# Seven block products in eight of the 22 row pairs of two down projections, with a later load and fewer dummies

## The chip, the cores and the metric

The kernel runs on one core of a Trainium2 chip. The metric is the device time of one execution in microseconds (us), as the median of several runs. TensorE (PE) multiplies, VectorE (DVE), ScalarE (ACT) and GpSimd (POOL) do the elementwise work, SyncE (SP) issues the transfers.

## The reference

One decoder layer on x of 256 tokens by 1024 features, in float32:

```
x <- LN1(alpha*x + 0.5*FFN1(x))
x <- LN2(alpha*x + W_out(sum_b sigmoid(g_b(x)) * P_b(mixer_b(x))))
x <- LN3(alpha*x + 0.5*FFN2(x))
FFN(x) = (silu(x @ w_gate) * (x @ w_up)) @ w_down      # 1024 -> 2816 -> 1024
```

The three mixers are a sliding-window attention, a block-sparse attention that at this length looks at its own block alone, and a cross-attention into 256 memory tokens `mem`, whose keys and values are `mem @ w_mem_kv + b`. alpha is 2 to the power 1/4. The change touches both FFNs and the time at which `mem` is loaded.

## The kernel before

Every weight is loaded once, as a chunk of 128 partitions x 2048 columns (1 MB), in the order in which `plan` lists them: for each FFN eleven gate and up chunks in turn, then eleven down chunks; between the FFNs those of the mixers. Each float32 operand is split in two parts of the type float32r: ScalarE casts the high part (`split`, L131), VectorE subtracts it for the low part (L132). A product is three matmuls (`product`, L187 to L189): high x high, high x low, low x high. So a chunk passes through SP (L153), ScalarE, VectorE and PE. `weights(key, ahead)` loads up to six chunks ahead and cuts up to two ahead. Three staging tiles (`raws`) hold loaded chunks; four slots each of `whi` and `wlo` (`parts`) hold cut ones, and a slot is written again when PE has read it for the last time. The order on SP is the program's own; on the other engines a scheduler orders the instructions when the kernel is built, and each engine then runs its list in that order. Only the first chunk is in program order on all of them.

In the gate and up loop of `ffn` the weights are stationary and the tokens move: for each feature block k one matmul of 512 columns (both parts of x) at L209 and one of 256 at L211. `gated` makes h = silu(g) * u * 0.5, and h is split into `hh` and `hl`. Chunk 0 of FFN 1 is worked in five groups of k as its pieces land (`FIRST`); after the second group `keep_warm(20)` puts 20 matmuls on a zero tile (L263) into PE's order, as 44 do at the start of the kernel.

In the down stage (`per_token`) h is stationary and the weights move. A down chunk holds two feature rows j of 128 by 1024 columns; for each of two token tiles t (128 tokens) and each half of the columns, `product` adds to one PSUM bank: 2 x 2 x 2 x 3 = 24 matmuls of 512 columns. There are eight banks. In FFN 2 the second half of t = 1 is cut into two banks of 256 columns (`ends`). The last three chunks are held back, so that all of t = 0 is finished before t = 1; then `normalize` takes alpha * resid + bank (L402), the statistics (L404 to L411) and the affine part (L415, L419) while PE works on t = 1. After FFN 1 PE goes on with the keys of mem (chunk mk), a transpose of the normalised x1 into x1T, the values of mem (mv), another transpose, and the projections of x1T (qa0, qa1, v0 and on).

`mem` is loaded by `hook_2` in chunk 7 of FFN 1 through a staging tile of `raws`, and split into `memT`, which has the tags C and E. The tag X1 belongs to x1. In FFN 2 the gate and up products of chunks 0 and 1 come first, by another way, and their h is turned and split in `hook_lead` at chunk 3, so `ffn` starts at chunk 2.

Of the kernel before, what the change touches and what calls it, by code (L numbers as in the profile page):

```python
# [17 lines left out]
P = 128  # L18
# [17 lines left out]
def plan():  # L36
# [79 lines left out]
def hybrid_layer(ctx: ExitStack, tc: tile.TileContext, a: dict, out: bass.AP):  # L116
# [39 lines left out]
    def part_to(n):  # L156
        while done["part"] <= min(n, len(chunks) - 1):
            i = done["part"]
            load_to(i)
            raw, how = raw_of.pop(i), chunks[i][1]  # L160
            if how:
                t = "1" if how == "leadg" else "2"
                hi = acts.tile([P, 2048], F32R, name="lhi", tag="A" + t)
                lo = acts.tile([P, 2048], F32R, name="llo", tag="B" + t)
            else:
                hi = parts.tile([P, 2048], F32R, name="whi")
                lo = parts.tile([P, 2048], F32R, name="wlo")
# [3 lines left out]
            part_of[i] = (hi, lo)  # L171
            done["part"] += 1

    def weights(key, ahead=2):
# [141 lines left out]
    def per_token(keys, lhs, keep, after, ahead=2, between=None, ends=HALVES):  # L316
# [23 lines left out]
        for t in range(2):  # L340
# [7 lines left out]
            after(t, [(*c, ps) for c, ps in zip(spans[t], py[t])])  # L348

    def gated(g, u):  # L350

# [5 lines left out]

    def ffn(n, x, after, start=0, hooks={}, h=None, ends=HALVES):
        hh, hl = h or (halves("hh", ("A1", "A2")), halves("hl", ("B1", "B2")))
        for c in range(start, NC):  # L360
            if c in hooks:
# [4 lines left out]
            for ks in FIRST if n == 1 and c == 0 else [range(KD)]:  # L366
                for key in ("g", "u"):
# [9 lines left out]
                    if ks.stop == KD:  # L377
# [3 lines left out]
                        gu.append(v)  # L381
                if ks == FIRST[1]:
                    keep_warm(20)
            split(gated(*gu).rearrange("p (j s) -> p j s", s=S), hh(2 * c, 2), hl(2 * c, 2))
        per_token([("d", n, c) for c in range(NC)],
                  lambda k, t: (hh(k)[:, 0, tok(t)], hl(k)[:, 0, tok(t)]), 3, after, ahead=1, ends=ends)

# [6 lines left out]

    def normalize(t, pss, resid, put, k=1.0):

# [3 lines left out]
        for c0, c1, ps in pss:  # L400
            r = work.tile([P, 512], F32, name="r", tag="w")[:, : c1 - c0]
            nc.vector.scalar_tensor_tensor(r, resid[:, t, c0:c1], k * ALPHA, ps, op0=ALU.mult, op1=ALU.add)  # L402
            for c in range(c0, c1, unit):
# [19 lines left out]

    def norm_into(resid, dst, k=1.0):
        return lambda t, pss: normalize(t, pss, resid, lambda t, s, r: (dst[:, t, s], None), k)


    memT = pair_of("memT", ("C", "E"))
    x_sb = const.tile([P, 2, D], F32, name="x_sb", tag="X0")
# [12 lines left out]
    x1 = const.tile([P, 2, D], F32, name="x1_sb", tag="X1")  # L442
    x1T = tokens_of("x1T")
    ffn(1, x0T, norm_into(x_sb, x1), hooks={4: hook_1, 7: hook_2})


# [270 lines left out]
    def finish(t, pss):  # L717
        def put(t, s, r):
            return r, lambda: nc.sync.dma_start(out=out[0, tok(t), s], in_=r)
        normalize(t, pss, x2, put)  # L720

    ffn(2, x2T, finish, start=2, hooks={3: hook_lead}, h=h2, ends=((0, 512), (512, 768), (768, D)))
    for key in ("g", "u"):
# [31 lines left out]
```

## Time and profile before

| What | Value |
|---|---|
| Median of 3 runs | 580.24 us (580.15 to 580.31) |
| Profiled execution | 580.73 us, of which its span is 578.9 |
| PE busy | 568.6 us, 98% of the span |
| VectorE busy | 397.6 us, 69% |
| ScalarE busy | 309.5 us, 53% |
| HBM traffic | 187 GB/s over the span |

The span is the profiler's, from the first to the last instruction; the time of a run has a little more around it. A share of busy time is a mean over stages that differ; windows of single stages say what fills each.

### The profile page before, as it was taken

The page shows a single profiled execution, that of the slowest core. Times are in us where ns is not written, and L with a number is a line of the kernel's source. Part 1 is how long each engine was busy: PE and PEld are TensorE (multiplying, and loading weights), DVE is VectorE, ACT ScalarE, POOL GpSimd, SP SyncE. Part 2 cuts the span into 40 slices and gives each one's busy share as a digit, 9 for nine tenths or more (in the row PEclk, how much of TensorE's full clock was granted, in tenths as well). Part 3 has the DMA queues.
Part 4 walks back from the last instruction along what each step waited for, and adds up shares of the span by engine and source line. Part 5 has one row for each costly group of instructions (what it writes and reads, how often), then busy time and mean ns, then how long its engine had stood idle before and what let it go on. Part 6 is the DMA issues. An engine that isn't in the chain of part 4 may idle for free.

```text
span 578.9 us, 8791 instructions
## 1 busy us (share of the span) xinstructions
PE 568.6 (98%) x3470; PEld 505.9 (87%) x3470; DVE 397.6 (69%) x609; ACT 309.5 (53%) x543; POOL 23.6 (4%) x37
## 2 busy tenths in 40 slices
PE   8999999999999999999999999999999999999994
PEld 7888888888888998999999989888888888888884
DVE  5887667764446977698787677996667657654336
ACT  6884556644333653964975665643565554633300
POOL 2000000000000000000002022210000000000001
PEclk9999999999999999999999999999999999999998
DMA  8887647745553474084163554536554555545201
GB/s 272 309 301 289 239 170 282 267 157 212 197 174 142 146 278 158 3 341 167 29 232 110 215 188 175 218 145 254 192 208 166 198 190 177 216 151 213 74 1 72
DMA packets 18025, 108.98 MB, mean 188 GB/s; under 512 B 2112, under 2 KB 2368, under 8 KB 5696
## 3 DMA queue, kind: packets, MB, share of 16 engines
q1 hardware_dynamic: 17984, 108.43, 52.0%
q8 instruction: 27, 0.44, 0.3%
q14 instruction: 14, 0.11, 0.1%
HBM read 107.37 MB, written 1.05 MB: 187 GB/s over the span
## 4 chain that ended last, share of the span: by engine, by line
PE 93%; ACT 3%; DVE 2%; DMA 1%; issue 0%; POOLq 0%; SPq 0%; DVEq 0%
PE ps L209 29%; PE ps L187 15%; PE ps L188 15%; PE ps L189 15%; PE ps L211 15%; ACT whi L131 1%; ACT sc_b L551 1%; DMA raw<-in_w_dram 1%; PE ps L575 1%; PE ps L255 1%; DVE sc_b L535 0%; DVE m L540 0%; PE ps L528 0%; ACT gates L611 0%; DVE r L419 0%
## 5 line engine op out<-in xcount | busy, mean ns | idle before, releaser
L132 DVE TENSOR_TENSOR wlo<-raw,whi 128x512 fp32r<-128x512 f32 (+2 forms) x234 | 233.8, 1030 | 127.0 <-ACT whi L131 122.6
L131 ACT CAST whi<-raw 128x512 fp32r<-128x512 f32 (+2 forms) x234 | 196.6, 882 | 121.7 <-PE ps L189 59.7
L209 PE MATMUL ps<-x0T,whi 128*128 128x512 f32 x352 | 89.5, 393 | 1.0 <-ACT whi L131 1.0
L209 PEld LDWEIGHTS ps<-x0T,whi 128*128 128x128 f32 x352 | 62.9, 189 | 12.3 <-ACT whi L131 1.4
L188 PE MATMUL ps<-wlo,hh 128*128 128x512 f32 (+1 forms) x198 | 72.5, 366 | 0.0
L187 PE MATMUL ps<-whi,hh 128*128 128x512 f32 (+1 forms) x198 | 72.5, 366 | 0.0
L189 PE MATMUL ps<-whi,hl 128*128 128x512 f32 (+1 forms) x198 | 72.3, 365 | 0.0
L209 PE MATMUL ps<-x2T,whi 128*128 128x512 f32 x288 | 72.2, 392 | 0.0
L209 PEld LDWEIGHTS ps<-x2T,whi 128*128 128x128 f32 x288 | 51.8, 189 | 9.3
L187 PE MATMUL ps<-x1T,whi 128*128 128x256 f32 x192 | 55.2, 287 | 0.3 <-ACT sc_m L551 0.3
L216 ACT COPY b<-ps 128x256 f32<-128x256 f32 x92 | 33.6, 368 | 39.6 <-PE ps L211 38.2
L188 PE MATMUL ps<-x1T,whi 128*128 128x256 f32 x192 | 54.3, 283 | 0.0
L189 PE MATMUL ps<-x1T,wlo 128*128 128x256 f32 x192 | 54.3, 283 | 0.0
L211 PEld LDWEIGHTS ps<-x0T,wlo 128*128 128x128 f32 x352 | 48.7, 190 | 4.2 <-DVE wlo L132 0.3
L211 PE MATMUL ps<-x0T,wlo 128*128 128x256 f32 x352 | 50.0, 282 | 0.0
L187 PEld LDWEIGHTS ps<-whi,hh 128*128 128x128 f32 x198 | 37.3, 188 | 6.1
L189 PEld LDWEIGHTS ps<-whi,hl 128*128 128x128 f32 x198 | 37.2, 188 | 6.2
L188 PEld LDWEIGHTS ps<-wlo,hh 128*128 128x128 f32 x198 | 37.3, 188 | 6.0
L211 PEld LDWEIGHTS ps<-x2T,wlo 128*128 128x128 f32 x288 | 39.3, 190 | 2.8
L211 PE MATMUL ps<-x2T,wlo 128*128 128x256 f32 x288 | 40.2, 282 | 0.0
L187 PEld LDWEIGHTS ps<-x1T,whi 128*128 128x128 f32 x192 | 36.8, 191 | 0.8 <-ACT sc_m L551 0.5
L188 PEld LDWEIGHTS ps<-x1T,whi 128*128 128x128 f32 x192 | 36.8, 192 | 0.0
(173 smaller groups left out, 762.8 us busy)
## 6 DMA issues: line engine op xcount, KB each, us to landing
raw<-in_w_dram SPq DMA_DIRECT2D x92, 1024.0 KB, 4.8
raw<-in_w_dram SPq DMA_DIRECT2D x16, 256.0 KB, 5.4
ln<-in_ln_dram SPq DMA_DIRECT2D x3, 1024.0 KB, 6.9
xT<-in_xT_dram SPq DMA_DIRECT2D x4, 256.0 KB, 6.5
x_sb<-in_x_dram SPq DMA_DIRECT2D x1, 1024.0 KB, 8.4
raw<-in_memT_dram SPq DMA_DIRECT2D x1, 1024.0 KB, 4.8
out_dram<-r SPq DMA_DIRECT2D x3, 256.0 KB, 2.1
brow<-in_by_column_dram SPq DMA_DIRECT2D x1, 387.0 KB, 8.5
```

What stands on the lines that cost most here:

```text
L131: nc.scalar.copy(hi, src)
L132: return nc.vector.tensor_sub(lo, src, hi.bitcast(F32))
L187: nc.tensor.matmul(ps, lh, rh, start=first and i == 0, stop=False)
L188: nc.tensor.matmul(ps, lh, rl, start=False, stop=False)
L189: nc.tensor.matmul(ps, ll, rh, start=False, stop=last and i == n - 1)
L209: nc.tensor.matmul(ps, wk, x.both[:, k], start=k == 0, stop=False)
L211: nc.tensor.matmul(ps[:, S:], wk, x[0][:, k], start=False, stop=k == KD - 1)
L216: nc.scalar.copy(b, ps[:, S:])
L255: nc.tensor.transpose(ps[:, j * P : (j + 1) * P], src[:, k * P : (k + 1) * P], ident)
L551: nc.scalar.activation(sc[:, e, c0:c1], raw[e][:, c0:c1], AF.Exp, bias=negm[:, e, t : t + 1], scale=SCALE, accum_out=ssum[:, e, t : t + 1])
L575: nc.tensor.transpose(pt[:, s * n + j * P : s * n + (j + 1) * P], sc[:, 2 * i + s, c : c + P], ident)
```

## The change

Four down chunks of each FFN (`SEVEN`: those that stand first, third, fifth and seventh in the order `DOWN`) are computed in the manner of Strassen: a chunk is a product of 2 x 2 blocks (two token tiles by two feature rows; two feature rows by two column halves), and seven block products of sums take the place of eight. The sums of h (s1 to s4) are made in the gate loop from h of that chunk and split into tiles with the tags C and E. The sums of the weights are made in `seven_parts` in a tile `t` with the tag X1 and split into a second pair of `whi` and `wlo` slots. The products are added up in banks 1 to 7; the plain chunks use banks 2, 3, 4 and x. After the eighth chunk the banks 1, 5, 6, 7 and x are added to alpha * resid (`settle`), and the last three chunks go on in banks 2, 3, 4 and new ones, so that `normalize` multiplies by 1 instead of alpha. FFN 2 works its down chunks in the order 2, 0, 4, 1, 6, 3, 8, 5, 7, 9, 10. `mem` is loaded after the eighth down chunk of FFN 1 into a tile with the tag X1, and split into tiles C and E when the sums of h are no longer read; x1 takes X1 after it. The 20 dummies in chunk 0 go. The 44 at the start stay.

```diff
+DOWN = {1: list(range(NC)), 2: [2, 0, 4, 1, 6, 3, 8, 5, 7, 9, 10]}
+SEVEN = (0, 2, 4, 6)
+KEEP = 3
...
-        for c in range(NC):
-            chunks.append((("d", n, c), None, rows(f"ffn{n}_w_down", c * 256)))
+        for i, c in enumerate(DOWN[n]):
+            chunks.append((("d", n, c), "seven" if i in SEVEN else None, rows(f"ffn{n}_w_down", c * 256)))
...
+            if how == "seven":
+                part_of[i] = seven_parts(raw)
+                done["part"] += 1
+                continue
...
+    def seven_parts(raw):
+        (bh, bl), (th, tl) = [tuple(parts.tile([P, 2048], F32R, name=nm) for nm in ("whi", "wlo")) for _ in range(2)]
+        t = const.tile([P, 2048], F32, name="t", tag="X1")
+        f = lambda v: v.rearrange("p (f c) -> p f c", f=2)
+        nc.vector.tensor_sub(f(t[:, :1024]), raw.rearrange("p (j f c) -> p j f c", j=2, f=2)[:, :, 1, :], f(raw[:, :1024]))
+        nc.vector.tensor_sub(t[:, 1024:1536], raw[:, 1536:], t[:, 0:512])
+        nc.vector.tensor_sub(t[:, 1536:], raw[:, 1024:1536], t[:, 1024:1536])
+        for o in (slice(0, 512), slice(1024, 2048)):
+            split(raw[:, o], bh[:, o], bl[:, o])
+        split(t, th, tl)
+        return (bh, bl), (th, tl)
...
+    def down(n, lhs, sums, resid, after, between=None, ends=HALVES):
+        order = DOWN[n]
+        bank = {b: acc.tile([P, 512], F32, name="ps") for b in (1, 6, 5, 7, 2, 3, "x", 4)}
+        n7, n8 = len(SEVEN), len(order) - KEEP - len(SEVEN)
+        left = {b: n7 for b in (1, 5, 6, 7)} | {b: n7 + 2 * (n8 + KEEP) for b in (2, 3, 4)} | {"x": 2 * n8}
+        fresh = set(bank)
+        def into(b, l, r):
+            left[b] -= 1
+            product(bank[b], [(l, r)], first=b in fresh, last=left[b] == 0)
+            fresh.discard(b)
+        def part(c, w, t, spans):
+            for j in range(2):
+                for b, (c0, c1) in spans:
+                    into(b, lhs(2 * c + j, t), two(w, ALL, slice(j * D + c0, j * D + c1)))
+        held = []
+        for i, c in enumerate(order):
+            w = weights(("d", n, c), 1 if i >= len(order) - KEEP else 2)
+            if i in SEVEN:
+                (s1, s2, s3, s4), (b, t) = sums[c], w
+                q = lambda x, o: two(x, ALL, slice(o * 512, (o + 1) * 512))
+                a11, a12, a22 = lhs(2 * c, 0), lhs(2 * c + 1, 0), lhs(2 * c + 1, 1)
+                for k, l, r in ((1, a11, q(b, 0)), (2, a12, q(b, 2)), (3, s4, q(b, 3)), (5, s1, q(t, 0)), (7, s3, q(t, 1)),
+                                (6, s2, q(t, 2)), (4, a22, q(t, 3))):
+                    into(k, l, r)
+            elif i < len(order) - KEEP:
+                for t in range(2):
+                    part(c, w, t, [((2, 3), (4, "x"))[t][f : f + 1] + (HALVES[f],) for f in range(2)])
+            else:
+                held.append((c, w))
+            if i == len(order) - KEEP - 1:
+                def more(x, ps):
+                    y = work.tile([P, 512], F32, name="y", tag="w")
+                    nc.vector.tensor_add(y, x, ps)
+                    return y
+                def settle(t, cs, u):
+                    nc.vector.scalar_tensor_tensor(resid[:, t, cs], resid[:, t, cs], ALPHA, u, op0=ALU.mult, op1=ALU.add)
+                lo, hi = (slice(*h) for h in HALVES)
+                e = work.tile([P, 512], F32, name="e", tag="w")
+                nc.scalar.copy(e, bank[1])
+                settle(0, lo, e)
+                u2 = more(e, bank[6])
+                settle(0, hi, more(u2, bank[5]))
+                u3 = more(u2, bank[7])
+                settle(1, lo, u3)
+                settle(1, hi, more(more(u3, bank[5]), bank["x"]))
+                if between:
+                    between()
...
+        for t in range(2):
+            for c, w in held[:-2]:
+                part(c, w, t, spans[t])
+            for sp in spans[t]:
+                for c, w in held[-2:]:
+                    part(c, w, t, [sp])
+            after(t, [(*cs, bank[b]) for b, cs in spans[t]])
...
-                if ks == FIRST[1]:
-                    keep_warm(20)
...
+            if c in sevens:
+                a11, a21, a12, a22 = (y[:, tok(i)] for i in range(4))
+                s = work.tile([P, 512], F32, name="s", tag="w")
+                s1, s2, s3, s4 = (s[:, tok(i)] for i in range(4))
+                nc.vector.tensor_add(s1, a21, a22)
+                nc.vector.tensor_sub(s3, a11, a21)
+                nc.vector.tensor_sub(s2, s1, a11)
+                nc.vector.tensor_sub(s4, a12, s2)
...
+                split(s.rearrange("p (i c) -> p i c", c=P), both[:, 0], both[:, 1])
...
-        raw = raws.tile([P, 2048], F32, name="raw")
+    def load_mem():
+        raw = const.tile([P, 2048], F32, name="mem", tag="X1")
         nc.sync.dma_start(out=raw, in_=a["memT"])
-        split(raw, *(t.rearrange("p k s -> p (k s)") for t in memT))
+        late["memT"] = pair_of("memT", ("C", "E"))
+        split(raw, *(t.rearrange("p k s -> p (k s)") for t in late["memT"]))
```

## Rows read from the trace of the kernel before

**Rows 1.** The page: busy time of PE, and the chain that ended last, by engine.

```profile
PE 568.6 (98%) x3470; PEld 505.9 (87%) x3470; DVE 397.6 (69%) x609; ACT 309.5 (53%) x543; POOL 23.6 (4%) x37
...
PE 93%; ACT 3%; DVE 2%; DMA 1%; issue 0%; POOLq 0%; SPq 0%; DVEq 0%
```

**Rows 2.** Windows: stretch, its length, busy time (instructions) of each engine, granted clock, DMA.

```profile
60.00:130.00 70.00, 70.00 (x403) 61.62 (x402) 48.81 (x52) 38.95 (x50) 0.00 (x0) 1.00 0.60 221
130.77:190.63 59.86, 59.86 (x266) 49.56 (x265) 32.62 (x43) 22.57 (x34) 0.98 (x1) 1.00 0.49 174
170.00:190.00 20.00, 20.00 (x90) 16.56 (x89) 13.33 (x23) 6.16 (x12) 0.98 (x1) 1.00 0.34 126
190.00:210.00 20.00, 20.00 (x168) 19.88 (x167) 19.48 (x37) 12.30 (x26) 0.99 (x1) 1.00 0.55 193
509.87:570.85 60.98, 60.98 (x332) 52.87 (x330) 28.08 (x26) 15.94 (x11) 0.92 (x1) 1.00 0.31 111
9.50:10.60 1.10, 1.10 (x22) 1.10 (x21) 1.10 (x3) 1.01 (x3) 0.00 (x0) 1.00 1.05 406
```

**Rows 3.** PE's timeline of the first down stage: start, duration, instruction.

```profile
130.77 0.40 PE L187 MATMUL ps<-whi,hh 128*128 128x512 f32 x1
...
190.63 0.28 PE L187 MATMUL ps<-memT,whi 128*128 128x256 f32 x1
190.75 0.28 PE L188 MATMUL ps<-memT,whi 128*128 128x256 f32 x1
```

**Rows 4.** Timelines of PE, ScalarE and VectorE in the first 31 us.

```profile
0.99 4.13 PE L263 MATMUL ps<-idle 128*128 128x128 bf16 x44 [0.99 <-DVE half L239]
...
7.09 0.73 PE L209 MATMUL ps<-x0T,whi 128*128 128x512 f32 x2 [0.56 <-ACT whi L131]
...
9.45 1.29 PE L263 MATMUL ps<-idle 128*128 128x128 bf16 x20
10.55 1.17 PE L209 MATMUL ps<-x0T,whi 128*128 128x512 f32 x4
...
19.03 2.00 PE L209 MATMUL ps<-x0T,whi 128*128 128x512 f32 x8
...
30.21 2.00 PE L209 MATMUL ps<-x0T,whi 128*128 128x512 f32 x8
...
9.02 1.27 ACT L131 CAST whi<-raw 128x512 fp32r<-128x512 f32 x2
...
9.02 0.69 DVE L132 TENSOR_TENSOR x0T<-xT,x0T 128x512 fp32r<-128x512 f32 x1 [0.52 <-ACT x0T L131]
9.67 1.35 DVE L132 TENSOR_TENSOR wlo<-raw,whi 128x512 fp32r<-128x512 f32 x2
```

**Rows 5.** VectorE's timeline at the start of the first down stage.

```profile
134.16 0.42 DVE L217 TENSOR_TENSOR u<-ps,b 128x256 f32<-128x256 f32 x1
```

**Rows 6.** Groups by line and form, VectorE and ScalarE, 130 to 200 us: busy, mean ns.

```profile
L132 DVE TENSOR_TENSOR wlo<-raw,whi 128x512 fp32r<-128x512 f32 x30 | 19.0, 683 | 13.6 <-ACT whi L131 13.6
L132 DVE TENSOR_TENSOR wlo<-raw,whi 128x2048 fp32r<-128x2048 f32 x4 | 9.2, 2293 | 10.3 <-ACT whi L131 10.3
...
L402 DVE SCALAR_TENSOR_TENSOR r<-x_sb,ps 128x512 f32<-128x512 f32 x4 | 2.7, 684 | 3.6 <-PE ps L189 3.6
...
L131 ACT CAST whi<-raw 128x2048 fp32r<-128x2048 f32 x4 | 7.6, 1912 | 9.0 <-PE ps L189 7.5 <-PE ps L209 1.5
```

**Rows 7.** Timelines of ScalarE and VectorE, cuts in the first down stage.

```profile
136.43 1.91 ACT L131 CAST whi<-raw 128x2048 fp32r<-128x2048 f32 x1 [0.40 <-PE ps L189]
...
169.73 2.50 DVE L132 TENSOR_TENSOR wlo<-raw,whi 128x512 fp32r<-128x512 f32 x4 [2.94 <-ACT whi L131]
```

**Rows 8.** The page's DMA issues: count, size, us to landing.

```profile
raw<-in_w_dram SPq DMA_DIRECT2D x92, 1024.0 KB, 4.8
```

**Rows 9.** Timelines of VectorE and PE where x1T is first read.

```profile
202.32 0.68 DVE L132 TENSOR_TENSOR x1T<-ps,x1T 128x512 fp32r<-128x512 f32 x1
...
203.87 0.28 PE L187 MATMUL ps<-x1T,whi 128*128 128x256 f32 x1
```

More of the change, by code (lines that the diff above doesn't have):

```diff
@@ L348, in per_token @@
             after(t, [(*c, ps) for c, ps in zip(spans[t], py[t])])
+    def down(n, lhs, sums, resid, after, between=None, ends=HALVES):
[45 more added lines that the diff above has]
+                    between()
+        for f in range(1, len(ends)):
+            bank["y", f] = acc.tile([P, 512], F32, name="ps")[:, : ends[f][1] - ends[f][0]]
+            left["y", f] = 2 * KEEP
+            fresh.add(("y", f))
+        spans = ([(2, HALVES[0]), (3, HALVES[1])], [(4, HALVES[0])] + [(("y", f), ends[f]) for f in range(1, len(ends))])
+        for t in range(2):
[5 more added lines that the diff above has]
+            after(t, [(*cs, bank[b]) for b, cs in spans[t]])
@@ L356, in gated, with ffn @@
         return h
-    def ffn(n, x, after, start=0, hooks={}, h=None, ends=HALVES):
+    def ffn(n, x, resid, after, start=0, hooks={}, h=None, between=None, ends=HALVES):
         hh, hl = h or (halves("hh", ("A1", "A2")), halves("hl", ("B1", "B2")))
+        sevens = [DOWN[n][i] for i in SEVEN]
+        pairs = [acts.tile([P, 2, 2, 4, P], F32R, name=f"s{i}", tag=t) for i, t in enumerate(("C", "E"))]
+        sums = {}
         for c in range(start, NC):
@@ L381, in ffn @@
                         gu.append(v)
-                if ks == FIRST[1]:
-                    keep_warm(20)
-            split(gated(*gu).rearrange("p (j s) -> p j s", s=S), hh(2 * c, 2), hl(2 * c, 2))
-        per_token([("d", n, c) for c in range(NC)],
-                  lambda k, t: (hh(k)[:, 0, tok(t)], hl(k)[:, 0, tok(t)]), 3, after, ahead=1, ends=ends)
+            y = gated(*gu)
+            split(y.rearrange("p (j s) -> p j s", s=S), hh(2 * c, 2), hl(2 * c, 2))
+            if c in sevens:
[6 more added lines that the diff above has]
+                nc.vector.tensor_sub(s4, a12, s2)
+                i = sevens.index(c)
+                both = pairs[i // 2][:, i % 2]
+                split(s.rearrange("p (i c) -> p i c", c=P), both[:, 0], both[:, 1])
+                sums[c] = [(both[:, 0, m], both[:, 1, m]) for m in range(4)]
+        down(n, lambda k, t: (hh(k)[:, 0, tok(t)], hl(k)[:, 0, tok(t)]), sums, resid, after, between, ends)
     ln = acts.tile([P, 2 * D], F32, name="ln")
@@ L393, in gains, with normalize @@
         broadcast(ln, a["ln"][n - 1 : n, :])
-    def normalize(t, pss, resid, put, k=1.0):
+    def normalize(t, pss, resid, put, k=1.0, scale=ALPHA):
         unit = min(c1 - c0 for c0, c1, _ in pss)
@@ L401, in normalize @@
             r = work.tile([P, 512], F32, name="r", tag="w")[:, : c1 - c0]
-            nc.vector.scalar_tensor_tensor(r, resid[:, t, c0:c1], k * ALPHA, ps, op0=ALU.mult, op1=ALU.add)
+            nc.vector.scalar_tensor_tensor(r, resid[:, t, c0:c1], k * scale, ps, op0=ALU.mult, op1=ALU.add)
             for c in range(c0, c1, unit):
@@ L422, in normalize, with norm_into @@
         return last
-    def norm_into(resid, dst, k=1.0):
-        return lambda t, pss: normalize(t, pss, resid, lambda t, s, r: (dst[:, t, s], None), k)
-    memT = pair_of("memT", ("C", "E"))
+    def norm_into(resid, dst, k=1.0, scale=ALPHA):
+        return lambda t, pss: normalize(t, pss, resid, lambda t, s, r: (dst[:, t, s], None), k, scale)
     x_sb = const.tile([P, 2, D], F32, name="x_sb", tag="X0")
@@ L437, in hook_2, with norm1 @@
         gains(1)
-        raw = raws.tile([P, 2048], F32, name="raw")
+    late = {}
+    def load_mem():
+        raw = const.tile([P, 2048], F32, name="mem", tag="X1")
         nc.sync.dma_start(out=raw, in_=a["memT"])
-        split(raw, *(t.rearrange("p k s -> p (k s)") for t in memT))
-    x1 = const.tile([P, 2, D], F32, name="x1_sb", tag="X1")
+        late["memT"] = pair_of("memT", ("C", "E"))
+        split(raw, *(t.rearrange("p k s -> p (k s)") for t in late["memT"]))
+    def norm1(t, pss):
+        if "x1" not in late:
+            late["x1"] = const.tile([P, 2, D], F32, name="x1_sb", tag="X1")
+        norm_into(x_sb, late["x1"], scale=1.0)(t, pss)
+    ffn(1, x0T, x_sb, norm1, hooks={4: hook_1, 7: hook_2}, between=load_mem)
+    memT, x1 = late["memT"], late["x1"]
     x1T = tokens_of("x1T")
-    ffn(1, x0T, norm_into(x_sb, x1), hooks={4: hook_1, 7: hook_2})
     km = tuple(const.tile([P, 2, S], F32R, name=f"km{i}") for i in range(2))
@@ L719, in put @@
             return r, lambda: nc.sync.dma_start(out=out[0, tok(t), s], in_=r)
-        normalize(t, pss, x2, put)
-    ffn(2, x2T, finish, start=2, hooks={3: hook_lead}, h=h2, ends=((0, 512), (512, 768), (768, D)))
+        normalize(t, pss, x2, put, scale=1.0)
+    ffn(2, x2T, x2, finish, start=2, hooks={3: hook_lead}, h=h2, ends=((0, 512), (512, 768), (768, D)))
     for key in ("g", "u"):
```

## The prediction

> **What bounds the kernel now.** I read the page's engine shares first, then the chain that ended last: TensorE holds 98% of the span and 93% of the chain [rows 1]. The windows by stage say the same of both down stages: 59.86 and 60.98 us with PE filling all of them at a granted clock of 1.00 [rows 2]. In PE's timeline the matmuls of the first down stage follow each other without a wait, from 130.77 to 190.63 us [rows 3]; 11 chunks x 24 products fill it, so one 512-column matmul costs 59.86 / 264 = 0.2267 us of path (a row shows 0.40 us for one, since neighbours overlap; the step from start to start is what counts). A 256-column matmul steps by 0.12 us [rows 3]. VectorE is the next engine: 33 of 60 us in this stage, but 19.5 of the 20 us that follow it [rows 2]. So: fewer matmuls shorten the path at once, and the reader is to look at what the added VectorE work does at the exit of stage one.
>
> **Removed matmuls.** A chunk as seven block products issues 7 x 3 = 21 matmuls of 512 columns where 24 stood. FFN 1: four chunks x 3 x 0.2267 = 2.72 us. FFN 2 before is 198 wide and 132 half-wide matmuls (the second half of the second token tile was cut in two all along): 198 x 0.2267 = 44.9, the rest of 60.98 is 16.1, or 0.122 for a half-wide one. After, only its last three chunks are cut so: 180 + 54 wide and 36 half-wide = 53.05 + 4.39 = 57.44 us, 3.54 less. Together 6.26 us. Stationary loads fall one for one with the matmuls, so nothing moves there. The Trainium skill (TensorE: Matmul & The Clock Gate, Back-to-back issue gap) gives about 131 ns for a 512-column matmul in a stream of loads and matmuls; by that the 24 wide ones would be worth 3.1 us instead of 5.4, and the sum would end at 576.3. The row shows 227 ns, so I do not use it.
>
> **Dummies.** The 20 dummies hold PE from 9.45 to 10.55 us [rows 4]. What the next real matmul reads is there earlier: the high part of the gate weights from 9.65 (first half of ScalarE's two casts at 9.02, 1.27 us for both), the low part of x0T at 9.02 + 0.69 = 9.71 [rows 4]. Bounds: 0 (if a later piece binds) and 1.10 us (the whole stretch). The low part of the gate piece, the first of two operations at 9.67, is there at 10.34, and PE, starting 0.8 earlier, wants it at 10.7; the later pieces keep this beat, so I take 0.8 us. PE has no idle time after that for 180 us, so the head start lasts.
>
> **VectorE and ScalarE in the gate and up stage.** For four chunks of each FFN: four sums of 128 columns (nearest row: 256 columns, 0.42 us [rows 5], an upper bound) and one split of 512 columns (0.69 on VectorE, 0.64 on ScalarE [rows 4]) = at most 2.4 us more on VectorE. It is busy 48.8 of 70 us there [rows 2], 7.8 per chunk of 30.21 - 19.03 = 11.18 us [rows 4]; 10.2 still fits, so nothing; if that cover were gone, 2.4 us a chunk.
>
> **Cutting the weights of a seven chunk.** VectorE before: one 2048-column subtraction, 2.29 us. After: sums of 1024, 512 and 512 columns, and low parts of 512, 1024 and 2048. With 0.683 for 512 and 2.293 for 2048 columns [rows 6], 1024 is about 1.22: 2.59 + 4.19 = 6.78 us. ScalarE: 1.91 becomes 0.62 + 1.05 + 1.91 = 3.58. Seven and plain chunks alternate: a pair costs VectorE 6.78 + 2.29 = 9.07 us while PE takes (21 + 24) x 0.2267 = 10.20. It fits with 1.1 us to spare if the handoffs overlap. The two buffer pairs of a seven chunk take two of the four slots, so I followed the slots: before, ScalarE's cast waits for PE to free the slot of the chunk four back [rows 7]; after, a seven chunk frees its slots one by one, the one with the raw quarters after 9 of its 21 matmuls (2.04 us), and by these releases and the durations above each chunk's last low part is written about 4 us before PE reads it. The staging tile for sums is single; its next user starts when the low part of 2048 columns is written, and its 2.59 us of sums end about 1.3 us before its own slots come free. I cost it at nothing; an uncovered part costs one for one.
>
> **Banks.** The stage starts with all eight PSUM banks. The bank of the fourth quadrant product is the slot of the last up tile, read at 134.16 + 0.42 = 134.58 us, 3.8 us into the stage [rows 5]; its first matmul is the 19th, 18 x 0.2267 = 4.1 us in. Before, a 2.29 us operation stood in front of that read; after, the pieces there are 1.2 us at most. Zero, with 1 us as the upper bound.
>
> **Settling and the late mem load.** Nine VectorE operations of 512 columns (0.684 each on PSUM [rows 6]) = 6.2 us and one ScalarE copy, once per FFN. Four of the five banks that they read are finished with the last seven chunk and the fifth 24 matmuls (5.4 us) later, so they run under one plain chunk and the last three (4 x 5.44 = 21.8 us of PE). The normalisation then multiplies by 1.0 instead of alpha: no change. In FFN 2 no weights of a next stage wait to be cut, and VectorE is busy only 28 of that stage's 61 us [rows 2]; nothing. In FFN 1 mem's low part (2048 columns, 2.29 us) comes into the same stretch: 8.5 us more work. VectorE is idle 20.00 - 13.33 = 6.7 us in the last 20 us of that stage, so 1.8 us spill into 190 to 210, where it is all but full [rows 2]. What is late next is x1T: its last low part ends at 203.00 and PE starts on it at 203.87 [rows 9], 0.87 us of slack. So 1.8 - 0.9 = 0.9 us of stall. Bounds: 0 (the weight cuts in that stretch are for chunks that PE reads later, and could give way) and 8.5 - 0.9 = 7.6 (all of it in front). I take 0.9.
> The mem transfer is queued on SP behind the load six chunks ahead, which waits for the cut of the last down chunk; that cut ends about 39 us into the stage by the slots above (172.23 - 130.77 = 41.5 before [rows 7]). Loads land 4.8 us after issue [rows 8]; issued near 39.5 and with two others in flight, mem lands near 47 (an estimate), is cut by 51 to 54, and PE reads it at 252 x 0.2267 = 57.1. Behind the waiting load on SP stand only later weights, which have the same wait today. x1 takes mem's staging place, so the first x1 write waits to about 54 too; its transposes come behind 48 half-wide matmuls, at 57.1 + 5.8 = 62.9. Zero, with 3 us of cover; if gone, one for one.
>
> **Sum.** -6.26 - 0.8 + 0.9 = -6.2 us. The profiled execution took 580.73 us (span 578.9 and 1.83 around it), 0.49 above the median 580.24: 574.5 for such an execution, 574.0 for a median.
>
> **The rivals.**
> 1. The exit of stage one costs more: the norm, mem and the cuts for the next two chunks meet in one in-order queue. For it: two windows full of VectorE work. Against: the cuts have lead. At half of its bound, 4 us: 580.2 - 7.1 + 4 = 577.1.
> 2. Mem lands late and PE waits at the exit with nothing else to do. For it: it stands behind a load that waits. Against: some 10 us between landing and use. 5 us beyond the cover: 574.0 + 5 = 579.
> 3. Slower: VectorE's beat overtakes PE's in the down stages, by the handoff from ScalarE in each pair. Each exposed 2048-column cast is 1.91 us [rows 6]; the spare is 1.1 us a pair, and the gain is 7.1 / 8 = 0.9 us a pair, so it decides from 2.0 us of exposed handoff a pair. With both casts of a pair exposed: 9.07 + 3.82 - 10.20 = 2.7 us x 8 pairs = 21.5, less a head start of 4 us a stage: 13.5, giving 586.6. For it: before, VectorE stood 2.94 us before a low part for its cast [rows 7]. Against: those casts lead PE by a whole chunk, and VectorE has other work meanwhile.
> 4. The clock falls in the first chunk. The 20 dummies come at 1.10 / 20 = 0.055 us each, against 4.13 / 44 = 0.094 for the 44 that open the kernel [rows 4], so this kernel shows a slow start; PE waits up to 0.56 us between the first groups [rows 4], and the granted clock around the dummies is 1.00 [rows 2]. If PE ran at the lower level from 9.45 to the end of the chunk at 19.03, the matmuls of 10.55 to 19.03, 8.5 us, would take double: 574.0 + 8.5 = 582.5; half of that stretch: 578.2. Against: after the dummies go PE idles 0.3 us, less than the waits before it that cost no clock. [...]
>
> **How the numbers follow.** Forecast 574.0 with its own range of 573.0 to 575.5 (exit 0 to 2.4 us): 0.62. Rival 1: 0.20 (575.5 to 579). Rival 2: 0.07. Rival 3: 0.06. Rival 4: 0.05. The range of 8 in 10 goes from 572.4 (nothing lost at the exit, 1.1 us from the dummies, half a us unseen) to 578.0, which takes in the forecast and most of rival 1. About 0.2% (1.2 us, 579.1 to 581.4) is what a measurement can tell from none. Faster: 0.62 + 0.19 + 0.05 + 0.03 = 0.89. Same: 0.04, from rivals 2, 3 and 4 where they just eat the gain. Slower: 0.07, mostly rival 3.
>
> **What the profile after would show.** Down stages of about 57.2 and 57.4 us with 252 and 270 matmuls and PE full; the second chunk's first matmul at about 18.2 instead of 19.03 us; VectorE near 54 of 57 us in stage one; mem's low part some 6 us before the first matmul on it; PE waits at x1T of a us or less. Wrong would be: PE waits on low parts inside a down stage (rival 3), on mem (2), on x1T or the mem weights for several us (1), or a granted clock below 1.00, or 512-column steps near 0.45 us, before 20 us (4).

## The result and the profile after

The changed kernel takes 574.0 us in the median of four runs (573.77 to 574.15), against 580.25 us (580.15 to 580.31) for the kernel before. The ratio is 0.989 with an interval of 0.9875 to 0.9909: faster by 1.1%. The forecast was 574.0.

The profiled execution took 573.77 us and its span is 572.0 us, 6.9 us less than the 578.9 before. The page shows the busy time of each engine and, below it, the chain that ended last by engine; these rows answer to [rows 1].

```profile
PE 561.8 (98%) x3378; PEld 498.3 (87%) x3378; DVE 452.7 (79%) x707; ACT 326.2 (57%) x569; POOL 23.6 (4%) x37
...
PE 92%; ACT 3%; DVE 2%; DMA 1%; issue 0%; SPq 0%; POOLq 0%; DVEq 0%
```

PE lost 92 instructions (12 matmuls in the first down stage, 60 in the second, 20 dummies) and stayed the bound; VectorE took on 98 instructions and 55 us and did not become it. That is the first thing to read: 98% of the span as before, and 92% of the chain against 93%, around a smaller amount of work.

The windows of the changed kernel, with stretch, its length, busy time of PE, PEld, DVE, ACT and POOL (instructions), granted clock, DMA share and GB/s, answer to [rows 2]. They are the gate and up stage, the first down stage, its last 20 us, the 20 us behind it, the second down stage, and the stretch where the dummies were.

```profile
60.00:130.00 70.00, 70.00 (x403) 61.62 (x402) 52.69 (x69) 38.64 (x54) 0.00 (x0) 1.00 0.54 199
129.84:187.02 57.18, 57.18 (x255) 47.33 (x254) 48.98 (x61) 31.35 (x42) 0.98 (x1) 1.00 0.59 217
167.00:187.00 20.00, 20.00 (x90) 16.53 (x90) 17.67 (x28) 8.00 (x14) 0.98 (x1) 1.00 0.59 233
187.00:207.00 20.00, 19.97 (x168) 19.77 (x166) 19.69 (x38) 11.96 (x24) 0.99 (x1) 1.00 0.38 136
506.49:563.90 57.41, 57.41 (x272) 48.18 (x270) 45.84 (x48) 22.90 (x18) 0.92 (x1) 1.00 0.38 134
8.00:18.00 10.00, 9.50 (x55) 8.15 (x54) 8.88 (x15) 8.79 (x16) 0.00 (x0) 1.00 0.92 334
```

PE fills both down stages as before, and each is shorter by the matmuls taken out. The last 20 us of the first one hold 17.67 us of VectorE work where 13.33 stood, and the 20 us behind it are full on both engines.

To see where each microsecond went I cut every run at five places in PE's timeline: the first matmul of the second chunk (c2), the first matmul of each down stage (d1, d2), the first on mem (mk) and the first on x1T (qa0). The last column is the median of the runs. All are us.

| kernel | start to c2 | c2 to d1 | d1 to mk | mk to qa0 | qa0 to d2 | d2 to its end | median |
|---|---|---|---|---|---|---|---|
| before | 19.03 | 111.74 | 59.86 | 13.24 | 306.00 | 60.98 | 580.25 |
| changed | 18.11 | 111.73 | 57.15 | 13.53 | 305.97 | 57.41 | 574.0 |
| difference | -0.92 | -0.01 | -2.71 | +0.29 | -0.03 | -3.57 | -6.25 |

So the whole difference lies in four places: the start, the two down stages, and 0.29 us given back in the stretch between mk and qa0. The spans differ by 6.9 and the medians by 6.25, because the profiled execution before was 0.48 above its median and the one after 0.23 below. One profiled execution further on, that of the experiment e12b, took 1977 us against 572.07 to 572.90 us in its three other runs; it is left out, and e12b has no stage times.

The start, in PE's timeline of the changed kernel and in VectorE's; the bracket is idle time and what ended it [rows 4].

```profile
8.72 0.40 PE L233 MATMUL ps<-x0T,wlo 128*128 128x256 f32 x2
9.62 1.16 PE L231 MATMUL ps<-x0T,whi 128*128 128x512 f32 x4 [0.50 <-DVE x0T L137]
...
18.11 2.02 PE L231 MATMUL ps<-x0T,whi 128*128 128x512 f32 x8
```

```profile
8.78 0.69 DVE L137 TENSOR_TENSOR x0T<-xT,x0T 128x512 fp32r<-128x512 f32 x1 [0.77 <-ACT x0T L136]
```

Where the dummies stood PE now waits 0.50 us for the low part of x0T. The granted clock of this stretch is 1.00, and the matmuls from there to the second chunk take 18.11 - 9.62 = 8.49 us, as the 19.03 - 10.55 = 8.48 before: no matmul became slower.

The 0.29 us are seen by following mem from issue to use. First the transfer's issue, in the timeline of SP's queue (the first row is three loads; the last of them leaves the queue at 163.89 + 10.54 = 174.43):

```profile
163.89 10.54 SPq L158 DMA_DIRECT2D raw<-in_w_dram  x3
174.48 0.43 SPq L546 DMA_DIRECT2D mem<-in_memT_dram  x1
```

Then VectorE's timeline around the settling (L410 and L414), ScalarE's cast of mem, and PE's first matmuls on it:

```profile
166.19 0.68 DVE L414 SCALAR_TENSOR_TENSOR x_sb<-x_sb,e 128x512 f32<-128x512 f32 x1
166.79 0.68 DVE L410 TENSOR_TENSOR y<-e,ps 128x512 f32<-128x512 f32 x1
167.39 0.68 DVE L137 TENSOR_TENSOR wlo<-raw,whi 128x512 fp32r<-128x512 f32 x1
168.00 1.27 DVE L410 TENSOR_TENSOR y<-y,ps 128x512 f32<-128x512 f32 x2
...
172.80 0.68 DVE L414 SCALAR_TENSOR_TENSOR x_sb<-x_sb,y 128x512 f32<-128x512 f32 x1
173.40 3.09 DVE L137 TENSOR_TENSOR wlo<-raw,whi 128x512 fp32r<-128x512 f32 x5
...
185.07 2.29 DVE L137 TENSOR_TENSOR memT<-mem,memT 128x2048 fp32r<-128x2048 f32 x1
...
182.95 1.91 ACT L136 CAST memT<-mem 128x2048 fp32r<-128x2048 f32 x1
...
186.99 0.40 PE L209 MATMUL ps<-memT,whi 128*128 128x256 f32 x2
187.42 0.39 PE L210 MATMUL ps<-memT,whi 128*128 128x256 f32 x1
187.64 0.28 PE L211 MATMUL ps<-memT,wlo 128*128 128x256 f32 x1
```

The four quarters of the last down chunk are cut at 167.39, 170.99, 172.20 and 173.40, with settling operations between them. Only when the fourth is done, at 173.40 + 0.68 = 174.08, does the load that waits for that buffer leave SP's queue, and mem, queued behind it, is issued at 174.48. The page gives 8.4 us from its issue to its landing:

```profile
mem<-in_memT_dram SPq DMA_DIRECT2D x1, 1024.0 KB, 8.4
```

It lands at 182.9, is cast until 184.86, and its low part ends at 185.07 + 2.29 = 187.36. PE starts on mem's high part at 186.99; the row holds two matmuls, so by steps of 0.12 it would want the low part at 187.23. Its first matmul on it is the row at 187.42, 0.19 later, and the next one follows after 0.22 in place of 0.12. Together these are the 0.29 us.

### The profile page after: what moved, and what is told of

It is laid out like the page before. It is cut to its first block, busy times and chain, and to the rows that moved or that the text cites. A ratio compares the mean times of both kernels' runs of the same rounds, so it can differ in the third digit from the quotient of the medians.

```text
span 572.0 us, 8735 instructions
## 1 busy us (share of the span) xinstructions
PE 561.8 (98%) x3378; PEld 498.3 (87%) x3378; DVE 452.7 (79%) x707; ACT 326.2 (57%) x569; POOL 23.6 (4%) x37
## 4 chain that ended last, share of the span: by engine, by line
PE 92%; ACT 3%; DVE 2%; DMA 1%; issue 0%; SPq 0%; POOLq 0%; DVEq 0%
PE ps L231 29%; PE ps L210 15%; PE ps L209 15%; PE ps L211 15%; PE ps L233 15%; ACT whi L136 1%; DMA xT<-in_xT_dram 1%; ACT sc_b L664 1%; PE ps L688 1%; PE ps L277 1%; DVE sc_b L648 1%; DVE m L653 0%; PE ps L641 0%; ACT gates L724 0%; DVE r L523 0%
## 5 line engine op out<-in xcount | busy, mean ns | idle before, releaser
L137 DVE TENSOR_TENSOR wlo<-raw,whi 128x512 fp32r<-128x512 f32 (+3 forms) x242 | 230.2, 983 | 64.1 <-ACT whi L136 57.7
L136 ACT CAST whi<-raw 128x512 fp32r<-128x512 f32 (+3 forms) x242 | 194.0, 845 | 96.8 <-PE ps L211 39.7
L210 PE MATMUL ps<-wlo,hh 128*128 128x512 f32 (+1 forms) x142 | 54.0, 380 | 0.0
L209 PE MATMUL ps<-whi,hh 128*128 128x512 f32 (+1 forms) x142 | 54.0, 380 | 0.0
L211 PE MATMUL ps<-whi,hl 128*128 128x512 f32 (+1 forms) x142 | 54.0, 380 | 0.0
L211 PEld LDWEIGHTS ps<-x1T,wlo 128*128 128x128 f32 x192 | 36.8, 191 | 0.0
L209 PEld LDWEIGHTS ps<-whi,hh 128*128 128x128 f32 x142 | 26.7, 188 | 5.1
L210 PEld LDWEIGHTS ps<-wlo,hh 128*128 128x128 f32 x142 | 26.7, 188 | 5.1
```

What stands on the lines that cost most here:

```text
L136: nc.scalar.copy(hi, src)
L137: return nc.vector.tensor_sub(lo, src, hi.bitcast(F32))
L209: nc.tensor.matmul(ps, lh, rh, start=first and i == 0, stop=False)
L210: nc.tensor.matmul(ps, lh, rl, start=False, stop=False)
L211: nc.tensor.matmul(ps, ll, rh, start=False, stop=last and i == n - 1)
```

## The experiments

### The dummies

Two kernels: the changed one with its dummies back, and the kernel before without them.

```diff
 (e1: the changed kernel)
+                if ks == FIRST[1]:
+                    keep_warm(20)
 (e10: the kernel before)
-                if ks == FIRST[1]:
-                    keep_warm(20)
```

> The changed kernel with the 20 dummies put back in the first chunk. My theory: PE was free to go on at 9.75 us and the dummies held it until 10.55, so they cost 0.8 us (0.4 to 1.1): 574.4 to 575.1 beside 574.0, with the second chunk's first matmul 0.4 to 1.1 us later than 18.11. Rival (they fill a wait for data and hold the clock up): no change or a gain, 573.0 to 574.1.

> The kernel before with the 20 dummies taken out and nothing else. Theory: PE is held by them only as long as they outlast the landing of x0T's third piece. In the profile of before they held it 0.69 us longer than that, in the changed kernel with the dummies put back 0.22 us, with the landing itself moving by 0.8 us from run to run: 0.2 to 0.7 us off, 579.6 to 580.1. Rival (they hold the clock up): steps of 512-column matmuls near 0.45 us before 18 us, and 581 or more.

Measured: with the dummies back 574.99 us (574.30 to 575.87), 1.0 over the changed kernel, but its own runs spread over 1.6 us; the kernel before without them 579.99 us (579.27 to 580.74), 0.3 under the kernel before beside it, with a ratio of 0.9985 to 1.0002 that takes in no change. The times alone do not settle a term of 0.8 us. PE's and VectorE's timelines say more; first those of the changed kernel with the dummies, then those of the kernel before without.

```profile
9.11 0.69 DVE L137 TENSOR_TENSOR x0T<-xT,x0T 128x512 fp32r<-128x512 f32 x1 [1.03 <-ACT x0T L136]
...
9.08 1.29 PE L285 MATMUL ps<-idle 128*128 128x128 bf16 x20
10.18 1.17 PE L231 MATMUL ps<-x0T,whi 128*128 128x512 f32 x4
```

```profile
8.72 0.69 DVE L132 TENSOR_TENSOR x0T<-xT,x0T 128x512 fp32r<-128x512 f32 x1 [0.64 <-ACT x0T L131]
...
9.55 1.17 PE L209 MATMUL ps<-x0T,whi 128*128 128x512 f32 x4 [0.26 <-DVE x0T L132]
...
18.03 2.00 PE L209 MATMUL ps<-x0T,whi 128*128 128x512 f32 x8
```

Without dummies PE waits for the low part of x0T, and the second chunk starts a fixed time after VectorE began that low part: 18.11 - 8.78 = 9.33 in the changed kernel, 18.03 - 8.72 = 9.31 here, and 9.31 to 9.33 in the nine other traces without dummies that are read here. With dummies it starts 19.03 - 9.02 = 10.01 us after it in the kernel before and 18.65 - 9.11 = 9.54 in e1. So the dummies held PE for 0.2 to 0.7 us in these two traces, not the 0.8 of the forecast. The rest of the 0.92 us between the two profiles is the moment at which the piece of x0T itself is there: VectorE began on it between 8.72 and 9.61 us (e2) over these runs, without regard to the change. Nothing became slower where the dummies went: rival 4 is out.

### The seven products alone

The changed kernel with all chunks as plain products: the late mem load, the missing dummies and the order of the chunks stay, the settling shrinks to the scaling of the residual and one bank.

```diff
+SEVENS = {1: (), 2: ()}
...
-        bank = {b: acc.tile([P, 512], F32, name="ps") for b in (1, 6, 5, 7, 2, 3, "x", 4)}
+        bank = {b: acc.tile([P, 512], F32, name="ps") for b in (2, 3, "x", 4)}
...
+                for t, cs in ((0, lo), (0, hi), (1, lo)):
+                    nc.vector.tensor_scalar(resid[:, t, cs], resid[:, t, cs], ALPHA, None, op0=ALU.mult)
+                settle(1, hi, bank["x"])
```

> The changed kernel with all eight plain down products in each FFN: its order of banks, the settling (three scalings and one sum), the late mem load, the missing dummies and the half-wide products only in the last three chunks all stay. Theory: the 24 matmuls are worth 24 x 0.2267 = 5.4 us, less 0.3 for the wait on mem, which goes when VectorE has less to do: 579.1 (578.9 to 579.5), with 264 and 282 matmuls in the down stages. Rival 1 (weight loads set the pace at 0.19 us each): 578.3 or less. Rival 2 (sums and settling cost PE some time unseen): less than 578.

Measured: 578.74 us (578.58 to 579.27), 0.2 under the range put down for it; the profiled execution, 579.27, lies inside. The down stages take 59.87 and 60.12 us. Against the changed kernel the seven products are worth 59.87 - 57.15 = 2.72 us in the first stage and 60.12 - 57.41 = 2.71 in the second: 12 matmuls of 0.2267 us each time. What is left of the second stage's gain, 60.98 - 60.12 = 0.86 us, is the part that the prediction found in the half-wide matmuls: before, all chunks cut the second half of the second token tile in two, now the last three alone. Mem lands in time here: with the shorter settling it is issued 172.07 - 130.21 = 41.9 us into the stage, its low part ends at 183.21, and PE comes to it at 190.08. From mk to qa0 it takes 13.23 us.

### The transfer of mem, and VectorE's load

Three kernels. One issues the mem transfer four chunks into the down stage, ahead of the loads that wait (only the issue moves; the cut keeps its place in the code). One computes the sums of the weights twice, 2.59 us more of VectorE for each seven chunk. One does both.

```diff
 (e2: the transfer earlier)
             w = weights(("d", n, c), 1 if i >= len(order) - KEEP else 2)
+            if i == 4 and early:
+                early()
...
+    def fetch_mem():
+        late["raw"] = const.tile([P, 2048], F32, name="mem", tag="X1")
+        nc.sync.dma_start(out=late["raw"], in_=a["memT"])
...
 (e4: the three sums of seven_parts twice; e9: e2 and e4)
+        for _ in range(2):
```

> The changed kernel with the transfer of mem issued after the fifth down chunk instead of the eighth; it is split at the same place as before. In the changed kernel mem is issued at 174.48, lands at 182.9, its low part ends at 187.36 and PE waits for it from 187.1 to 187.42. Theory A (the queue on SP sets the low part of mem): the low part ends by 183 at the latest, that wait of 0.3 us goes, and the time falls by 0.3 us to 573.7. Theory B (VectorE is full there, and order on it sets the loss): the wait moves to x1T, which had 0.15 us of slack (200.37 to 200.52), and the time stays within 0.1 us of the changed kernel.

> The changed kernel with the three sums of the weights made twice, so that a seven chunk costs VectorE 9.4 us instead of 6.8 and a pair of chunks 11.7 us against 10.2 us of PE. If VectorE's beat sets the down stages from there on, 8 pairs x 1.5 us = 11.7 us less the lead of about 4 us a stage: 577 to 582, with PE waits on low parts. Rival (the sums are made in time that VectorE stands idle, and the first chunk's before the stage): less than 1 us more, 574.0 to 575.0. Where it is between, the exit of the first stage should show the wait first.

> The sums of the weights made twice, as in the run with 581.0 us, and mem's transfer issued after the fifth down chunk. With the sums twice, the first stage and the stretch behind it lost 2.8 + 3.6 us against the changed kernel, all of it in waits on memT (2.2 on its cast, 2.1 on its low part among them), and the second down stage only 0.4. Theory A (the queue on SP, which mem shares with loads that wait for VectorE's cuts, made the loss): memT is ready long before, and most of the 6.4 us come back: 575 to 576. Theory B (VectorE's backlog itself made it): the waits move to x1T or to the low parts of the next chunks, and the time stays over 578.

| kernel | d1 to mk | mk to qa0 | qa0 to d2 | d2 to its end | median |
|---|---|---|---|---|---|
| changed | 57.15 | 13.53 | 305.97 | 57.41 | 574.0 |
| e2, mem earlier | 57.14 | 13.24 | 305.98 | 57.41 | 573.97 |
| e4, sums twice | 59.96 | 17.15 | 305.96 | 57.81 | 581.04 |
| e9, both | 57.58 | 13.23 | 306.59 | 57.86 | 574.9 |

With the transfer issued at 160.44 in place of 174.48, mk to qa0 is 13.24 us again, as before the change: the 0.29 us are the wait on mem and nothing else. They are too few to show in the medians (573.62 to 574.36).

The sums twice are the harder test. A pair of chunks now costs VectorE 9.07 + 2.59 = 11.7 us against PE's 10.2, which is the condition of rival 3. The time rose by 7.0 us, to 581.04. But PE's timeline, from the first down stage to x1T, has three waits of more than 0.1 us, and the two long ones are at mem:

```profile
190.30 0.50 PE L210 MATMUL ps<-memT,whi 128*128 128x256 f32 x2 [2.21 <-ACT memT L136]
192.87 0.48 PE L211 MATMUL ps<-memT,whi 128*128 128x256 f32 x1 [2.06 <-DVE memT L137]
```

The reason stands in SP's queue, where five loads ahead of mem hold it for 19.67 us:

```profile
160.31 19.67 SPq L158 DMA_DIRECT2D raw<-in_w_dram  x5
180.03 0.43 SPq L547 DMA_DIRECT2D mem<-in_memT_dram  x1
```

Behind the waits the granted clock fell too, in the window from the first of them to the first matmul on x1T, which is part of the 3.6 us lost there:

```profile
190.30:207.45 17.15, 15.09 (x112) 14.88 (x113) 15.87 (x27) 8.02 (x16) 0.99 (x1) 0.90 0.35 121
```

The third wait is 0.12 us, on the low part of a seven chunk's weights, and the stage lost 0.4 us around it; in the timeline of the weight loads into PE, whose bracket holds their own longer idle time, it is

```profile
164.65 0.19 PEld L211 LDWEIGHTS ps<-wlo,s 128*128 128x128 f32 x1 [0.55 <-DVE wlo L137]
```

This is the sign of rival 3, at a small price. The second stage, with the same work on VectorE but no transfer that the next stage needs, lost 0.40 us. And with mem ahead in the queue (e9) the same doubled sums cost 0.9 us between the medians: 6.1 of the 7.0 came back by moving one issue. In e9's trace 0.43 us are lost in the first stage, 0.45 in the second, and 0.62 at x1T, as PE's and then VectorE's timeline show:

```profile
200.76 0.64 PE L210 MATMUL ps<-x1T,whi 128*128 128x256 f32 x4
...
201.98 0.39 PE L211 MATMUL ps<-x1T,whi 128*128 128x256 f32 x1
```

```profile
201.23 0.69 DVE L137 TENSOR_TENSOR x1T<-ps,x1T 128x512 fp32r<-128x512 f32 x1
```

The low part that PE needs at 201.98 is done at 201.23 + 0.69 = 201.92. So VectorE's longer beat by itself costs about half a microsecond at each of three places; what costs more is that it delays a cut, by the cut a load, and by the load the transfer behind it.

### More chunks as seven products

A fifth seven chunk in the second stage, then in both, with mem early in each.

```diff
 (e6)
+SEVENS = {1: (0, 2, 4, 6), 2: (0, 2, 4, 6, 7)}
...
 (e8, mem issued at i == 5)
+SEVENS = {1: (0, 2, 4, 6, 7), 2: (0, 2, 4, 6, 7)}
...
 (both: the fifth chunk's sums of h in places of their own)
+        more = [tuple(const.tile([P, 4, P], F32R, name=f"more{i}{j}", tag=f"{t}{j}") for j in range(2))
+                for i, t in enumerate(("km", "vm")[: len(sevens) - 4])]
```

> The changed kernel with mem's transfer issued after the fifth down chunk, and a fifth seven chunk in FFN 2 (the eighth in its order; its sums of h lie in places that the mixers' keys had). Theory: three matmuls less, 0.68 us off the second down stage (57.41 to 56.73), and 0.3 us off the exit of the first: 573.0. Rival (two seven chunks in a row are too much for VectorE: 13.6 us of cuts for 9.5 us of PE): the last three chunks start late, the stage keeps its 57.4 us or more, and the time is 573.7 or more.

> As the run before, with a fifth seven chunk in FFN 1 too, and mem issued after the sixth down chunk. Theory A (PE alone counts while VectorE has any idle time): another 0.68 us off: 572.3. Theory B (VectorE is full from the fifth seven chunk to x1T, where 0.15 us were to spare, and has 4.5 us more to do): the first down stage takes 56.5 us, but PE waits 1 to 4 us behind it, so 573.5 to 576.5.

Measured: e6 572.93 us (572.83 to 573.28), ratio 0.9858 to 0.9887. Its second stage takes 56.72 us, 0.69 less: three matmuls. Its median is 1.1 us under that of the changed kernel, which was not run beside it; the two intervals overlap, but the trace shows the 0.69 us and the 0.30 us at mem. e8 gets nothing on top, 573.13 us (572.55 to 573.26): its first stage takes 56.98 us where three matmuls less would give 57.15 - 0.68 = 56.47, and qa0 to d2 is 0.3 longer, lost at the low part of x1T as in e9 (done at 201.10, where PE had come to x1T at 200.26). The loads of the weights into PE show the loss at the end of that stage, where the settling and the quarter cuts share VectorE; the bracket is the wait for the low part.

```profile
177.28 0.19 PEld L211 LDWEIGHTS ps<-wlo,hh 128*128 128x128 f32 x1 [0.56 <-DVE wlo L138]
178.49 0.19 PEld L211 LDWEIGHTS ps<-wlo,hh 128*128 128x128 f32 x1 [0.21 <-DVE wlo L138]
```

A sixth in the second stage makes four seven chunks in a row, where VectorE's work (6.78 us a chunk) is longer than PE's (4.76). Four kernels: with one staging tile for the sums as in the change (e7), with a second one in turns (e13), and both once more with the chunks in the order seven, seven, plain (e12, e12b).

```diff
 (e7: mem early)
+SEVENS = {1: (0, 2, 4, 6), 2: (0, 2, 4, 5, 6, 7)}
...
 (e13: e7 and)
...
-        t = const.tile([P, 2048], F32, name="t", tag="X1")
+        staged[0] += 1
+        pool, tag = (acts, "xT") if staged[0] in (8, 10) else (const, "X1")
+        t = pool.tile([P, 2048], F32, name="t", tag=tag)
...
 (e12, and with e13's edit e12b)
+SEVENS = {1: (0, 2, 4, 6), 2: (0, 1, 3, 4, 6, 7)}
+DOWN = {1: list(range(NC)), 2: [2, 3, 0, 4, 5, 1, 6, 7, 8, 9, 10]}
```

> Mem early, and six seven chunks in FFN 2, four of them in a row (fifth to eighth place). Theory (VectorE's beat now sets the stage): four in a row cost VectorE 27.1 us for 19.0 us of PE; with a lead of about 4 us some 4 us are waited, for 1.36 us of matmuls saved: 575 to 577. Rival (the lead is larger, or the plain chunks behind give it back): 572.3.

> The kernel with six seven chunks in FFN 2, four in a row, as in the run with 578.35 us, where the row went in a beat of 8.5 us a chunk: VectorE stood idle 2.05 us in each for the cast of the sums, and ScalarE waited for the next sums. Here the staging tile of the sums takes turns with the place of x2T, which is no longer read then. Theory (the one staging tile makes the beat): the idle time goes, the beat falls to 6.8 us, and the second down stage from 61.8 to 57 to 60 us: 573.5 to 576.5. Rival (the slots of the cut weights make the beat): the stage stays within 0.5 us of 61.8.

> Six seven chunks in FFN 2 in the order seven, seven, plain, three times less one plain (places 1, 2, 4, 5, 7, 8), with one staging tile and mem early. Two seven and one plain chunk are 15.0 us of PE; VectorE has 15.9 us for them, and 2.05 us more where the second of a pair waits for the staging tile with nothing else to do. If that wait is filled with the plain chunk's cut, the lead of about 4 us carries the stage: 56.1 us, 572.3. If not: 2.9 us x 2.7 less 4: 59 to 60 us, 575 to 576.

> The same with the staging tile taking turns with the place of x2T for the fourth and the sixth seven chunk. Theory: 0.9 us a triple is all that VectorE is behind, the lead carries it, and the second down stage takes 56.1 us: 572.3, the shortest of all. Rival: the slots of the cut weights set the pace, and it is no better than the run with one staging tile.

| kernel | second down stage | median | ratio, interval |
|---|---|---|---|
| e7, four in a row, one tile | 61.84 | 578.35 | 0.9951 to 0.9977 |
| e13, four in a row, two tiles | 56.44 | 572.86 | 0.9858 to 0.9885 |
| e12, spread, one tile | 62.08 | 578.30 | 0.9943 to 0.9973 |
| e12b, spread, two tiles | not read | 572.35 | 0.9848 to 0.9878 |

By its matmuls e7's stage would take 56.05 us (57.41 less six of 0.2267). It takes 61.84, and the 578.35 us are above both figures that I had put down. VectorE's and ScalarE's timelines, and PE's wait at the end, show a circle of two engines around the one tile:

```profile
526.60 0.69 DVE L191 TENSOR_TENSOR t<-raw,t 128x512 f32<-128x512 f32 x1
529.35 2.29 DVE L138 TENSOR_TENSOR wlo<-t,whi 128x2048 fp32r<-128x2048 f32 x1 [2.05 <-ACT whi L137]
...
537.89 2.29 DVE L138 TENSOR_TENSOR wlo<-t,whi 128x2048 fp32r<-128x2048 f32 x1 [2.05 <-ACT whi L137]
...
527.40 1.91 ACT L137 CAST whi<-t 128x2048 fp32r<-128x2048 f32 x1 [4.25 <-DVE t L191]
...
535.95 1.91 ACT L137 CAST whi<-t 128x2048 fp32r<-128x2048 f32 x1 [5.16 <-DVE t L191]
...
546.90 1.32 PE L210 MATMUL ps<-whi,more 128*128 128x512 f32 x3 [2.59 <-ACT whi L137]
```

VectorE writes t, ScalarE waits for it and casts it, VectorE waits 2.05 us for the cast to write the low part, and only then may t be written again: one turn is 537.89 - 529.35 = 8.54 us, against 4.76 us of PE, and the two engines idle in turns. PE, ahead at first, runs out at 546.90. With a second tile (e13, VectorE's timeline) VectorE does another chunk's work during the cast:

```profile
523.26 2.28 DVE L138 TENSOR_TENSOR wlo<-t,whi 128x2048 fp32r<-128x2048 f32 x1
...
530.11 2.29 DVE L138 TENSOR_TENSOR wlo<-t,whi 128x2048 fp32r<-128x2048 f32 x1 [0.23 <-ACT whi L137]
```

This turn is 6.85 us, nearly all of it VectorE's own work, the next two are 5.08 and 6.15 us, and the stage takes 56.44 us. The order of the chunks is not what counts: spread out but with one tile (e12) it is as slow as in a row, which went against both figures that I had put down for it. With two tiles both are shorter than with one, by 5.5 and 6.0 us, e12b as far as was expected and e13 further; between the two, and between them and e6, the intervals overlap. In the profiled execution of e13, the longest of its four (572.39 to 573.77 us), qa0 to d2 is 0.8 us longer than in the changed kernel. About 0.7 of it lies in the mixers from 275.1 to 277.2, where PE takes the transposes of sc_b as VectorE and ScalarE finish them; why they were late stays open.

## Why the prediction was right, point by point

The time and its sign were right, and so was the mechanism: PE bound the kernel, and its matmuls could be counted out of the path.

**Removed matmuls: right.** 2.72 and 3.54 us were forecast, 2.71 and 3.57 came; the experiment without seven products puts 2.72 + 2.71 on them and 0.86 on the half-wide matmuls. Reading the price from the step between neighbours, 0.2267 us, and not from one row's duration of 0.40, was what made the sum: 12 matmuls cost 2.72 us in this kernel. The Trainium skill (TensorE: Matmul & The Clock Gate, Back-to-back issue gap) gives about 131 ns for a 512-column matmul in a stream of loads and matmuls. This trace does not agree: it shows 227 ns, and the measurement decides.

**Dummies: right in kind, a little large.** 0.8 us was taken from a bound of 1.10; the traces give 0.2 to 0.7. The forecast let PE start 0.04 us after the low part of x0T was done (9.75 after 9.71); in the changed kernel it starts 0.15 after (9.62 after 8.78 + 0.69), which makes 0.69 of the 0.8. The second chunk started at 18.11 (18.2 forecast), helped by a piece of x0T that was there 0.24 us earlier than in the profile before.

**Sums of h in the gate and up stage: right.** VectorE is busy 52.69 of 70 us there in place of 48.81, and from the second chunk to the first down stage it takes 111.73 us as before.

**Cuts of the weights: right.** The operations of 1024 columns took 1.22 us as worked out. In VectorE's rows by form, from 130 to 187 us, they stand beside the two other sizes, which did not change [rows 6]:

```profile
L137 DVE TENSOR_TENSOR wlo<-raw,whi 128x512 fp32r<-128x512 f32 x25 | 15.9, 683 | 3.1 <-ACT whi L136 2.4 <-PE ps L233 0.8
L137 DVE TENSOR_TENSOR wlo<-t,whi 128x2048 fp32r<-128x2048 f32 x3 | 6.9, 2292 | 3.1 <-ACT whi L136 3.1
...
L137 DVE TENSOR_TENSOR wlo<-raw,whi 128x1024 fp32r<-128x1024 f32 x3 | 3.7, 1219 | 0.1
```

The exposed handoffs that rival 3 turned on are the 3.1 us in the second row, three waits of about 1 us, one for each cast of t in this stage: half of the 2.0 a pair from which it would have decided. VectorE was busy 49 us in the stage, not 54, as part of the first chunks' cuts is done ahead of it.

**Banks: right.** No wait was found.

**Exit of stage one: the step that failed.** The forecast put 0.9 us on x1T, with 1.8 us of VectorE work spilling over, and "zero, with 3 us of cover" on mem. It was the other way round. In the changed kernel x1T lost nothing: its low part ends at 200.37 and PE comes to it at 200.52.

```profile
199.09 1.28 DVE L137 TENSOR_TENSOR x1T<-ps,x1T 128x512 fp32r<-128x512 f32 x2
```

The slack of 0.87 us [rows 9] shrank to 0.15, so the spill was there, but it stayed inside the slack; e9 and e8 go over it, by 0.6 and 0.3 us. And the cover of mem was used up: issued 44.6 us into the stage in place of 39.5, because the settling stands between the quarter cuts of the last down chunk; 8.4 us under way in place of 7.5; low part done 57.5 us into the stage in place of 54. PE wanted it at 57.4. In e3, where the settling is shorter and the cuts are plain, the cover is 6.9 us. That is rival 2's mechanism at a price of 0.29 us; the run with the transfer moved shows it, and the run with doubled sums shows how near it was to 6 us. The prediction had the settling's 6.2 us in its sum of VectorE work but not in the date of the cut that lets SP's queue go on.

**Rival 1** did not come, **rival 3** not in the changed kernel (its mechanism, a beat made longer by handoffs, appears with a sixth seven chunk and one staging tile), **rival 4** not at all.

**The sum.** The differences of the table add up to 6.95 us, the 6.9 between the spans. Forecast were 6.2 between medians, and 6.25 was measured. The measured terms, -2.71 - 3.57 + 0.29 and 0.2 to 0.7 for the dummies, make -6.2 to -6.7, so the medians lie at the near end. Hitting the tenth is luck in part: the start moves by 0.9 us from run to run, and a dummies term that was too large stood beside a stall that was too large.

## What to carry to other kernels

Where PE fills its stage, price a removed matmul by the step from start to start, and then look for the cost not on the engine that takes on the work but at the transfers that queue behind its results. A load that waits for a buffer holds every later issue on its queue: put the transfer that the next stage needs ahead of such loads, and date it by the last operation that frees the buffer, with all that stands between on that engine. Before a chain of two engines through one staging tile is repeated closer together, give it a second tile; here that was worth 5.4 us of one stage, while the order of the chunks made no difference that the times show.

## What the runs showed of the hardware that I had not expected

- The start varies, and the stage behind it does not: over these runs VectorE began on the same piece of x0T between 8.72 and 9.61 us, while the 111.73 or 111.74 us from the second chunk to the first down stage came back in every trace.
- The same transfer of 1 MB took 4.8 us to land in the kernel before, 6.9 when issued at 160.44 (e2), and 8.4 in the changed kernel. In both of the later cases a weight load had been issued 0.38 us before it, so that alone does not make the difference; it stays open.
- A wait of PE costs more than its length. In e7 PE waited 2.59 us up to 546.90; the windows of 5 us from 545 on show the granted clock below full and back again:

```profile
545.00:550.00 5.00, 3.04 (x8) 1.99 (x9) 3.12 (x2) 5.00 (x3) 0.00 (x0) 0.73 0.62 210
550.00:555.00 5.00, 5.00 (x22) 4.08 (x22) 5.00 (x4) 2.27 (x2) 0.00 (x0) 0.93 0.00 0
555.00:560.00 5.00, 5.00 (x24) 4.14 (x23) 4.96 (x7) 0.00 (x0) 0.00 (x0) 1.00 0.00 0
```

The mean of 0.73 lies between the two levels, 1.2 and 2.4 GHz. The waits of 0.39 and 0.50 us in the first chunk of the changed kernel, with a granted clock of 1.00, cost no clock.
